# Attention products with v made feature-major in column halves of the array, and P divided by its sum before it is transposed

## The chip, the cores and the metric

The kernel runs on one core of a Trainium2 chip. The metric is the device time of one execution in microseconds (us). The engines are TensorE (PE in the profile, PEld its weight loads), VectorE (DVE), ScalarE (ACT), GpSimd (POOL) and SyncE (SP), which run their own queues of instructions in order and wait for each other by semaphores.

## What is computed

One sequence of 256 tokens, 1024 features wide, goes through three layers: a mixer that joins two attentions (MoBA with 8 heads, NSA with 8 heads in two groups), a squared-ReLU MLP, a forgetting attention ("fox") with 16 heads, a second MLP, and a hybrid layer (two SwiGLU blocks around differential attention and a state-space mixer). The change is in the first two mixers. Cut to what matters there, each head computes, with a bias table T that carries the causal mask:

```python
p = softmax(q @ k.T * scale + T)          # 256 x 256 per head, in two query blocks of 128
o = p @ v                                 # 256 x 64 per head
# NSA: three such products per head (compressed, selected, window keys),
#      o = g0 * o_cmp + g1 * o_slc + g2 * o_win, with gates g per token and head
# FoX: T[q, k] = cum[q] - cum[k], worked out in the kernel
y = concat(o of all heads) @ w_out
```

All of it is float32. Products with the streamed weights are made from a high and a low part of each factor (`whi`, `wlo`, and the halves of `xx`); the small products inside an attention are plain float32 matmuls, which the trace records as two passes each.

## The kernel before

A stream of weight pieces (`raw`, by SP's DMA queue) is split by ACT (`whi`, L387) and DVE (`wlo`, L388) while TensorE multiplies the piece before. A mixer is a generator `main` that makes its projections chunk by chunk, and a generator `attend2` that makes the attention; `drive` takes a step of the one and a step of the other, and a scheduler then orders each engine's queue by priorities that follow from that interleaving.

`attend2` treats heads by twos. There are 20 such pairs: 8 of NSA and 4 of MoBA in `even`, 8 in `fox`. A pair goes through these stages, each in another round of the loop:

- Age 0: four products of q and k into two PSUM banks (L214, `ps_b<-k,q`). The two heads' features lie in partitions 0 to 63 and 64 to 127, so the two heads use the two halves of the array's rows. DVE adds the table and finds the row's minimum of the negated scores (L542, into `S`), ACT makes the exponential and its sum (L545, `P` from `S`).
- Age 1: six transposes of P by TensorE (L555, three blocks of 128x128 a head, because the upper right block of 256x256 is masked), copied from PSUM to `PT` by ACT for the first head (L558) and by DVE for the second (L560).
- Age 2: products with v (L218, `ps_o<-v,PT`): P transposed is the stationary side, 128x128, and 64 columns of v move. Three such matmuls a head, six passes, so twelve passes a pair. The result is token-major: tokens in partitions, the heads side by side in a bank.

When all heads of a group are through, the sums are inverted, and DVE multiplies the outputs with them as it reads PSUM (`xn<-ps_o,mr`, L869 for NSA, where the gate is in the factor, L890 for MoBA, L1237 in `fox`; ten instructions of 128x512). For NSA, POOL adds the two parts (L878) and DVE the compressed one. The result is token-major and the output projection wants features in partitions, so `turn` transposes it by TensorE (L397, `ps_b<-cst,xn`, 32 blocks over both mixers) and splits it into high and low.

In `fox` the bias tables are built by POOL while the attention runs: for each of 16 heads four instructions (L1190, L1192, L1194, L1195) write a tile `S` out of a DMA-broadcast row (`T<-c_dram`) and the cumulated gates. `S` has four buffers and `P` five. `getT(h)` builds up to three tables ahead.

## Time and profile before

| | us |
|---|---|
| median of 3 runs (lowest, highest) | 1219.6 (1218.25, 1220.39) |
| the profiled execution | 1220.97 |
| its span in the trace | 1219.2 |
| busy in the span: PE, DVE, ACT, POOL | 1189.3, 785.6, 656.1, 119.0 |
| the first mixer's attention lies in | 36 to 142 of the span |
| the fox mixer's attention lies in | 367 to 475 of the span |

The span is what the trace covers from the first to the last instruction; the execution's own time has 1.8 us more around it. Ends of matmuls are modelled in the trace, and neighbours overlap, so what a group of matmuls costs is read from its first start to the start of what follows on TensorE, not from its duration.

### The profile page before, as it was taken

To read this page: it belongs to the slowest core of one execution; us is meant where nothing else is said; L and a number is where in the kernel's file an instruction comes from. 1 tells how busy PE (TensorE), PEld (TensorE's weight loads), DVE (VectorE), ACT (ScalarE), POOL (GpSimd) and SP (SyncE) were. 2 spreads that over 40 slices of the span, in tenths; PEclk is the share of its full clock that TensorE was granted. 3 is DMA by queue.
4 is the path that set the end of the run, shared out by engine and by line. 5 is a ranking of instruction groups with operands and counts; after the bars stand their busy time and mean duration, and the time that the engine had idled before them with its cause. 6 is when DMAs were issued, how large, how long until landed. Compare 5 with 4: busy or idle time off the path is not lost.

```text
span 1219.2 us, 17931 instructions
## 1 busy us (share of the span) xinstructions
PE 1189.3 (98%) x7008; PEld 1025.5 (84%) x7008; DVE 785.6 (64%) x1339; ACT 656.1 (54%) x1209; POOL 119.0 (10%) x182
## 2 busy tenths in 40 slices
PE   8999999999999999999999999999999999999997
PEld 6998888888887888888888888887988778988886
DVE  5676575656655546666676756576787876656563
ACT  6665454455454555545455555574664765555552
POOL 2001000000005220000002000002333120000000
PEclk9999999999999999999999999999999999999999
DMA  8645245555444424555563555562453235454550
GB/s 306 232 156 190 92 170 190 189 194 185 175 177 187 139 105 155 208 185 195 187 228 143 207 185 195 186 229 99 180 171 115 97 107 205 174 205 176 198 179 35
DMA packets 32533, 211.26 MB, mean 173 GB/s; under 512 B 3792, under 2 KB 4592, under 8 KB 8640
## 3 DMA queue, kind: packets, MB, share of 16 engines
q1 hardware_dynamic: 29040, 199.47, 46.0%
q0 software_dynamic: 3120, 10.38, 2.5%
q8 instruction: 55, 0.90, 0.3%
q10 hardware_dynamic: 288, 0.26, 0.1%
q14 instruction: 30, 0.25, 0.1%
HBM read 208.74 MB, written 1.09 MB: 172 GB/s over the span
## 4 chain that ended last, share of the span: by engine, by line
PE 84%; DVE 8%; ACT 4%; issue 2%; POOL 1%; DMA 1%; DVEq 0%; SPq 0%; ACTq 0%; POOLq 0%
PE ps_b L214 39%; PE ps_p L214 24%; PE ps_o L214 15%; DVE wlo L388 3%; PE ps_o L218 2%; ACT whi L387 1%; PE ps_p L397 1%; ACT P L545 1%; PE ps_b L397 1%; ACT xn L410 1%; PE ps_b L555 1%; DVE k L1326 1%; DVE xn L427 1%; POOL rs L416 1%; DMA gain<-in_mix_norm 1%
## 5 line engine op out<-in xcount | busy, mean ns | idle before, releaser
L388 DVE TENSOR_TENSOR wlo<-raw,whi 128x1024 fp32r<-128x1024 f32 (+1 forms) x365 | 447.8, 1245 | 245.6 <-ACT whi L387 244.7
L387 ACT ACTIVATE whi<-raw 128x1024 fp32r<-128x1024 f32 (+1 forms) x367 | 377.0, 1048 | 196.5 <-PE ps_p L214 90.4
L214 PE MATMUL ps_b<-xx,whi 128*128 128x512 f32 x1024 | 361.5, 394 | 0.0
L214 PE MATMUL ps_b<-xx,wlo 128*128 128x256 f32 x1024 | 289.0, 282 | 0.0
L214 PEld LDWEIGHTS ps_b<-xx,whi 128*128 128x128 f32 x1024 | 192.3, 188 | 43.8
L214 PEld LDWEIGHTS ps_b<-xx,wlo 128*128 128x128 f32 x1024 | 192.5, 188 | 1.7
L214 PE MATMUL ps_p<-xx,whi 128*128 128x256 f32 (+2 forms) x800 | 148.0, 287 | 1.2 <-ACT k L1324 0.7
L214 PEld LDWEIGHTS ps_p<-xx,whi 128*128 128x128 f32 (+2 forms) x800 | 121.9, 186 | 5.7 <-issue 3.1
L214 PE MATMUL ps_p<-xx,wlo 128*128 128x256 f32 x384 | 108.4, 282 | 0.0
L214 PE MATMUL ps_b<-whi,xx 128*128 128x256 f32 (+2 forms) x440 | 103.1, 321 | 0.0
L416 POOL TENSOR_TENSOR rs<-ms,mhalf 128x1 f32<-128x1 f32 x22 | 14.9, 675 | 825.9 <-DVE ms L423 825.9
L214 PE MATMUL ps_p<-whi,xx 128*128 128x512 f32 x232 | 83.8, 416 | 1.3 <-DVE xx L388 1.0
L214 PEld LDWEIGHTS ps_b<-whi,xx 128*128 128x128 f32 x440 | 73.2, 189 | 5.7 <-ACT xx L387 0.3
L214 PEld LDWEIGHTS ps_p<-xx,wlo 128*128 128x128 f32 x384 | 72.7, 189 | 0.0
L214 PE MATMUL ps_p<-whi,q 128*128 128x512 f32 x216 | 71.5, 391 | 0.0
L214 PE MATMUL ps_o<-whi,q 128*128 128x512 f32 x216 | 71.3, 391 | 0.0
L214 PE MATMUL ps_b<-wlo,xx 128*128 128x256 f32 (+2 forms) x220 | 70.6, 321 | 0.3 <-DVE wlo L388 0.2
L242 ACT ACTIVATE tB<-ps_b 128x256 f32<-128x256 f32 x128 | 47.7, 373 | 40.8 <-PE ps_b L214 40.8
L214 PE MATMUL ps_p<-whi,k 128*128 128x512 f32 x184 | 61.4, 394 | 0.0
L214 PE MATMUL ps_o<-whi,k 128*128 128x512 f32 x184 | 61.1, 393 | 0.0
L214 PEld LDWEIGHTS ps_p<-whi,xx 128*128 128x128 f32 x232 | 43.9, 191 | 15.0 <-issue 4.3
L387 ACT ACTIVATE k<-P 128x256 fp32r<-128x256 f32 x48 | 20.0, 418 | 64.2 <-DVE P L1054 36.8
(324 smaller groups left out, 1767.2 us busy)
## 6 DMA issues: line engine op xcount, KB each, us to landing
raw<-in_w_m SPq DMA_DIRECT2D x64, 1024.0 KB, 4.8
raw<-in_w_s SPq DMA_DIRECT2D x16, 1024.0 KB, 4.9
raw<-in_w_o SPq DMA_DIRECT2D x12, 1024.0 KB, 4.9
raw<-in_w_f1g SPq DMA_DIRECT2D x11, 1024.0 KB, 4.8
raw<-in_w_f1u SPq DMA_DIRECT2D x11, 1024.0 KB, 4.8
raw<-in_w_f1d SPq DMA_DIRECT2D x11, 1024.0 KB, 4.8
raw<-in_w_f2g SPq DMA_DIRECT2D x11, 1024.0 KB, 4.9
raw<-in_w_f2u SPq DMA_DIRECT2D x11, 1024.0 KB, 4.8
```

Source lines behind the costliest of these rows:

```text
L214: self.last_mm = self.nc.tensor.matmul(out, l, r, start=start, stop=stop)
L218: self.nc.tensor.matmul(out, l, r, start=start, stop=False, skip_group_check=True)
L242: nc.scalar.activation(tmp[:m], ps[:m, 256:512], AF.Copy)
L387: self.nc.scalar.activation(hi, src, AF.Copy)
L388: self.nc.vector.tensor_sub(lo, src, hi)
L397: i = self.nc.tensor.transpose(ps[:, k * 128:k * 128 + 128], src[:, (b + k) * 128:(b + k) * 128 + 128], self.ident)
L410: self.nc.scalar.activation(junk[:, h * 512:h * 512 + 512], halves[h], AF.Square, scale=1.0 / 32, accum_out=ss[:, h:h + 1])
L416: self.last_pow = self.nc.gpsimd.tensor_tensor(r, m, self.mhalf, op=OP.pow)
L427: self.nc.vector.scalar_tensor_tensor(dst, src, r, G, op0=OP.mult, op1=OP.mult)
L545: nc.scalar.activation(P[:, o:o + w], s[:, o:o + w], AF.Exp, scale=-1.0, bias=nm[:, j:j + 1], accum_out=J["sum"][:, j:j + 1])
L555: nc.tensor.transpose(b[:, c * 128:c * 128 + 128], P[:, c * 128:c * 128 + 128], self.ident)
L1326: nc.vector.scalar_tensor_tensor(xc[:, f], u[:, f, w:w + 256], cw[:, f, w:w + 1], xc[:, f], op0=OP.mult, op1=OP.add)
```

## The change

In both first mixers a pair's stages become:

- Age 0: as before, with DVE's minimum and ACT's exponential in place (`P` holds both; the two rings of buffers are joined to one of nine). The two heads' four sums lie in one tile `psum`; one RECIPROCAL on DVE makes `prec`. For NSA, POOL multiplies `prec` with the gate (128x4). Then four multiplications of P by its factor, two of 128x128 and two of 128x256: on POOL for the twelve pairs of `even`, on DVE for the eight of `fox`.
- Age 2 instead of 1: the transposes and copies.
- Age 3 instead of 2: products with v, v stationary (128x64), `PT` moving: 256 columns for the first block of keys (both query blocks at once) and 128 for the second. The first head writes PSUM partitions 0 to 63 and the second 64 to 127, which puts their stationary sides in the two halves of the array's columns. The order is: first head 256, second head 256, first head 128, second head 128. So four matmuls a pair, and the result is feature-major.

The outputs then need neither the division nor the turn: a new `take` splits them from PSUM straight into the high and low halves of `oT`. The compressed part of NSA accumulates in the same PSUM tile (four matmuls of 256 columns for two of 512). The ten `xn<-ps_o,mr`, POOL's two sums and the 32 transposes go. The rows of the output projection's weights are put in the new order of heads on the host before the launch. The diff, cut to its core:

```diff
-SB = 4
+PB = 9
+PAIR_T = 2
...
-            old = at.get(2)
+            old = at.get(PAIR_T + 1)
             if old:
                 flight.remove(old)
-                for J in old:
-                    pt, v, O = J["pt"], J["v"], J["O"]()
-                    s = slice(J["col"], J["col"] + 64)
-                    self.mmo(O[:, 0, s], pt[:, 0:128], v[0], J["first"])
-                    self.mmo(O[:, 1, s], pt[:, 128:256], v[0], J["first"])
-                    self.mmo(O[:, 1, s], pt[:, 256:384], v[1], False)
-                    if "after" in J:
-                        J["after"](pend)
+                O, c = old[0]["O"](), old[0]["col"]
+                for lo, n, i in ((0, 256, 0), (128, 384, 1)):
+                    for x, J in enumerate(old):
+                        o = O[64 * x:64 * x + 64, c // 512, c % 512 + lo:c % 512 + 256]
+                        self.mmo(o, J["v"][i], J["pt"][:, 256 * i:n], J["first"] and not i)
+                if "after" in old[0]:
+                    old[0]["after"]()
...
-                for J, b in zip(new, st):
+                sums = self.t([128, 2, 2], "psum", 3)
+                for x, (J, b) in enumerate(zip(new, st)):
...
-                    s = s0 if s0 is not None else self.t([128, 384], "S", SB)
-                    P = self.t([128, 384], "P", 5)
+                    P = J["P"] = s0 if s0 is not None else self.t([128, 384], "P", PB)
...
+                r = self.t([128, 2, 2], "prec", 3)
+                nc.vector.reciprocal(r, sums)
+                new[0]["norm"](r)
+                for x, J in enumerate(new):
+                    P = J["P"]
+                    for o, w, j in ((0, 128, 0), (128, 256, 1)):
+                        J["eng"].tensor_tensor(P[:, o:o + w], P[:, o:o + w],
+                                               r[:, x, j:j + 1].to_broadcast([128, w]), op=OP.mult)
             yield
-            for J in at.get(1, ()):
+            for J in at.get(PAIR_T, ()):
...
+    def take(self, O, oT, k, c, n=256):
+        m = n // 256
+        self.split(oT[:, k:k + m, 0:256], oT[:, k:k + m, 256:512],
+                   O[:, c // 512, c % 512:c % 512 + n].rearrange("p (k n) -> p k n", k=m))
...
         def nsa_sum():
-            for t in range(2):
-                o = no[t]
-                nc.gpsimd.tensor_tensor(o[:, :512], o[:, :512], o[:, 512:], op=OP.add)
-                ps = self.bank("p")
-                self.mm(ps, cpt[t][:120, :], vb[:120, :], True, True)
-                nc.vector.tensor_add(o[:, :512], o[:, :512], ps)
-                self.turn(o, oT, 4, t)
+            for j in range(4):
+                self.mmo(nO()[:, j // 2, j % 2 * 256:j % 2 * 256 + 256], vb[:120, j * 128:j * 128 + 128],
+                         w2[:120, 0:256], False)
+            for b in range(2):
+                self.take(nO(), oT, 4 + 2 * b, 512 * b, 512)
...
+                def norm(r, b=b, j=j):
+                    nc.gpsimd.tensor_tensor(r, r, gate.rearrange("p t (g j i) -> p j i g t", g=2, j=4)[:, j, b + 1],
+                                            op=OP.mult)
...
+                norm=lambda r: None, eng=nc.vector, first=h // 2 % 2 == 0, ev="av"[h % 2],
```

The scheduler then places the instructions anew. TensorE's queue at the third pair of NSA's products of q and k, where `xx` with `whi` and `wlo` are projections; before:

```order
L214 MATMUL ps_p<-xx,whi 128x256 x2
L214 MATMUL ps_p<-xx,wlo 128x256
L218 MATMUL ps_o<-v_157,PT 128x64 x6
L214 MATMUL ps_b<-k_156,q_155 128x128 x2
L214 MATMUL ps_b<-k_156,q_155 128x256 x2
```

and after:

```order
L215 MATMUL ps_p<-xx,wlo 128x256
L215 MATMUL ps_b<-k_156,q_155 128x128 x2
L219 MATMUL ps_o<-PT,v_157 64x256 x2
L219 MATMUL ps_o<-PT,v_157 64x128 x2
L215 MATMUL ps_b<-k_156,q_155 128x256 x2
L215 MATMUL ps_p<-xx,whi 128x256 x2
```

The pair's products with v, six matmuls that were whole, are four that stand inside the next pair's products of q and k. In 12 of the 20 pairs the two heads' 256 columns stand next to each other as here; in the other 8 something stands between them.

At the start of `fox`, TensorE's queue from the first pair's transposes (L555 before, L560 after) to the third pair's products of q and k; before:

```order
L555 MATMUL ps_b<-cst,P 128x128 x2
L214 MATMUL ps_p<-whi,xx 128x512
L218 MATMUL ps_o<-v_3232,PT 128x64 x6
L214 MATMUL ps_p<-whi,xx 128x512
L214 MATMUL ps_p<-wlo,xx 128x512
L214 MATMUL ps_p<-whi,xx 128x512
L214 MATMUL ps_b<-k_3231,q_3230 128x128
L218 MATMUL ps_o<-v_3232,PT 128x64 x6
```

and after:

```order
L215 MATMUL ps_p<-wlo,xx 128x512
L560 MATMUL ps_b<-cst,P 128x128 x5
L215 MATMUL ps_p<-whi,xx 128x512 x2
L219 MATMUL ps_o<-PT,v_3234 64x256
L560 MATMUL ps_b<-cst,P 128x128 x6
L215 MATMUL ps_p<-wlo,xx 128x512
L219 MATMUL ps_o<-PT,v_3234 64x256
L219 MATMUL ps_o<-PT,v_3234 64x128 x2
L215 MATMUL ps_p<-whi,xx 128x512
L215 MATMUL ps_b<-k_3233,q_3232 128x128 x2
```

Between the second pair's products of q and k and the first transpose there stood 48 passes of 256 columns, and now there stand 60 and four of 512; nine of 512 lie ahead of the third pair's products of q and k where six lay.

DVE's queue at the same place, behind the minima of the first two pairs (the last of them is the first row of each); before:

```order
L542 ISA S_3555,nm_3603<-ps_b_3592,S_3555 128x256
L542 ISA nm_3603 128x1
L560 COPY PT_3646<-ps_b_3642 128x384
L560 COPY PT_3695<-ps_b_3691 128x384
L388 TENSOR_TENSOR wlo_3730<-raw_3462,whi_3729 128x1024 x2
L542 ISA S_3604,nm_3751<-ps_b_3745,S_3604 128x128
```

and after:

```order
L542 ISA P_3556,nm_3609<-ps_b_3598,P_3556 128x256
L548 RECIPROCAL prec_3565<-psum_3534 128x4
L553 TENSOR_TENSOR P_3536<-P_3536,prec_3565 128x128
L553 TENSOR_TENSOR P_3536<-P_3536,prec_3565 128x256
L553 TENSOR_TENSOR P_3541<-P_3541,prec_3565 128x128
L553 TENSOR_TENSOR P_3541<-P_3541,prec_3565 128x256
L548 RECIPROCAL prec_3624<-psum_3603 128x4
L553 TENSOR_TENSOR P_3551<-P_3551,prec_3624 128x128
L553 TENSOR_TENSOR P_3551<-P_3551,prec_3624 128x256
L565 COPY PT_3687<-ps_b_3683 128x384
L389 TENSOR_TENSOR wlo_3723<-raw_3463,whi_3722 128x1024
```

Both pairs' multiplications (eight, of which six are shown) stand behind the minimum of the fourth head and ahead of the first copy of PT. POOL's queue goes on building tables through this stretch, as before.

## Rows read from the trace of the kernel before

**Rows 1.** The page: its head, the busy time of the engines, and the chain of work that ended last.

```profile
span 1219.2 us, 17931 instructions
PE 1189.3 (98%) x7008; PEld 1025.5 (84%) x7008; DVE 785.6 (64%) x1339; ACT 656.1 (54%) x1209; POOL 119.0 (10%) x182
...
PE 84%; DVE 8%; ACT 4%; issue 2%; POOL 1%; DMA 1%; DVEq 0%; SPq 0%; ACTq 0%; POOLq 0%
```

**Rows 2.** Windows: busy time of PE, PEld, DVE, ACT and POOL (us, with the number of instructions), granted clock, DMA share and GB/s in the two attention stretches.

```profile
36.00:142.00 106.00, 104.27 (x770) 90.78 (x769) 67.76 (x182) 58.85 (x156) 7.47 (x9) 1.00 0.44 156
367.00:475.00 108.00, 104.22 (x707) 89.97 (x705) 61.00 (x127) 55.79 (x128) 37.01 (x71) 0.98 0.38 137
```

**Rows 3.** Groups by line: the products with v on PE (48 of the 288 passes belong to the third mixer, which is not changed) and the turns of outputs (32 of the 64 go). Columns behind the bar: busy us, mean ns of one, then idle time just before.

```profile
L218 PE MATMUL ps_o<-v,PT 128*128 128x64 f32 x288 | 36.9, 272 | 1.5 <-ACT PT L558 1.5
L397 PE MATMUL ps_b<-cst,xn 128*128 128x128 f32 x64 | 10.0, 289 | 4.1 <-DVE xn L427 4.0
```

**Rows 4.** Timeline of PE in `fox`: a pair's products with v and its neighbours (start in us, duration with the modelled end, what, how many passes).

```profile
437.63 0.28 PE L214 MATMUL ps_p<-xx,wlo 128*128 128x256 f32 x1
437.75 1.45 PE L218 MATMUL ps_o<-v,PT 128*128 128x64 f32 x12
439.01 0.36 PE L214 MATMUL ps_p<-xx,whi 128*128 128x256 f32 x1
```

**Rows 5.** The same view: eight transposes of an output, and what follows.

```profile
455.46 1.04 PE L397 MATMUL ps_b<-cst,xn 128*128 128x128 f32 x8
456.25 0.47 PE L214 MATMUL ps_b<-whi,xx 128*128 128x512 f32 x1
```

**Rows 6.** The same view: a pair's products of q and k (eight passes, of two heads in the two halves of the rows), the projections before and behind, and six transposes of P.

```profile
427.46 0.40 PE L214 MATMUL ps_p<-xx,whi 128*128 128x256 f32 x2
427.70 0.28 PE L214 MATMUL ps_p<-xx,wlo 128*128 128x256 f32 x1
427.91 0.93 PE L214 MATMUL ps_b<-k,q 64*128 64x128 f32 x8
428.77 0.50 PE L214 MATMUL ps_p<-xx,whi 128*128 128x256 f32 x2
429.11 0.28 PE L214 MATMUL ps_p<-xx,wlo 128*128 128x256 f32 x1
...
430.30 0.82 PE L555 MATMUL ps_b<-cst,P 128*128 128x128 f32 x6
430.87 0.48 PE L214 MATMUL ps_p<-xx,whi 128*128 128x256 f32 x2
431.19 0.28 PE L214 MATMUL ps_p<-xx,wlo 128*128 128x256 f32 x1
```

**Rows 7.** The same view in `even`: six transposes, then products whose stationary side is only 60 or 30 columns wide.

```profile
58.20 0.82 PE L555 MATMUL ps_b<-cst,P 128*128 128x128 f32 x6
58.77 0.36 PE L214 MATMUL ps_p<-whi,gain 128*60 128x256 f32 x1
58.97 0.40 PE L214 MATMUL ps_p<-wlo,gain 128*30 128x256 f32 x2
59.20 0.28 PE L214 MATMUL ps_p<-whi,gain 128*60 128x256 f32 x1
```

**Rows 8.** One line's instructions, with the lowest, median and highest duration in ns, first and last start: splits by DVE that read two tiles of SBUF, POOL's first two instructions of a table, and DVE's copies of PT.

```profile
L388 DVE TENSOR_TENSOR wlo<-raw,whi x365: 731/1220/4497, 9.8 to 1192.0; 128x1024 fp32r<-128x1024 f32 x181, 128x560 fp32r<-128x560 f32 x1, 128x1120 fp32r<-128x1120 f32 x1
L388 DVE TENSOR_TENSOR k<-P,k x48: 414/425/426, 194.7 to 1188.6; 128x256 fp32r<-128x256 f32 x48
L388 DVE TENSOR_TENSOR whi<-raw,whi x2: 292/292/293, 353.9 to 858.1; 128x128 fp32r<-128x128 f32 x2
L1190 POOL TENSOR_TENSOR S<-T,cq x16: 388/398/1388, 380.4 to 432.7; 128x128 f32<-128x128 f32 x16
L1192 POOL TENSOR_TENSOR S<-T,cq x16: 602/608/1592, 381.3 to 434.0; 128x256 f32<-128x256 f32 x16
L560 DVE COPY PT<-ps_b x20: 495/555/559, 53.2 to 451.5; 128x384 f32<-128x384 f32 x20
```

**Rows 9.** Groups by line: ACT's exponentials and the readout of their sums (mean ns behind the comma).

```profile
L545 ACT ACTIVATE P<-S,nm 128x256 f32<-128x256 f32 x40 | 19.9, 497 | 2.7 <-DVE nm L542 2.5
...
L545 ACT ACTIVATION_READ_ACCUMULATOR P<-S,nm 128x1 f32 x80 | 15.0, 188 | 0.0
```

**Rows 10.** Timeline of DVE at the start of `fox`: the first and the last of the minima of the first four heads.

```profile
382.34 0.29 DVE L542 CUSTOM_DVE_ANT_0 S<-ps_b,S 128x128 f32<-128x128 f32 x1 [1.28 <-POOL S L1194]
...
388.02 0.42 DVE L542 CUSTOM_DVE_ANT_0 S<-ps_b,S 128x256 f32<-128x256 f32 x1
```

**Rows 11.** Timeline of PE at the same place: the last projection before the wait, the first transpose, and the third pair's products of q and k.

```profile
381.60 0.28 PE L214 MATMUL ps_p<-xx,wlo 128*128 128x256 f32 x1
383.33 0.30 PE L555 MATMUL ps_b<-cst,P 128*128 128x128 f32 x1 [1.45 <-DVE nm L542]
...
391.78 0.49 PE L214 MATMUL ps_b<-k,q 64*128 64x128 f32 x2
```

**Rows 12.** Windows of one us at the same place, columns as in Rows 2; the granted clock is the third figure from the end.

```profile
384.00:385.00 1.00, 0.43 (x3) 0.23 (x3) 0.73 (x4) 0.52 (x3) 1.00 (x4) 0.95 1.04 401
385.00:386.00 1.00, 0.91 (x5) 0.94 (x6) 0.15 (x1) 0.58 (x2) 1.00 (x3) 0.50 0.36 148
387.00:388.00 1.00, 1.00 (x7) 1.00 (x6) 0.30 (x2) 0.39 (x3) 1.00 (x4) 0.50 0.08 33
388.00:389.00 1.00, 1.00 (x5) 0.53 (x3) 0.90 (x3) 0.95 (x5) 1.00 (x3) 0.85 0.00 0
```

**Rows 13.** Timeline: a DVE split of two SBUF tiles while POOL builds tables without a break, and the last POOL instruction of that stretch.

```profile
391.61 4.50 DVE L388 TENSOR_TENSOR wlo<-raw,whi 128x1024 fp32r<-128x1024 f32 x1
394.57 0.45 POOL L1195 TENSOR_TENSOR S<-S,cst 128x128 f32<-128x128 f32 x1
```

**Rows 14.** Timeline: two DVE splits, and POOL's table instructions beside them, some us later.

```profile
402.10 3.02 DVE L388 TENSOR_TENSOR wlo<-raw,whi 128x1024 fp32r<-128x1024 f32 x2 [0.28 <-ACT whi L387]
402.09 0.40 POOL L1190 TENSOR_TENSOR S<-T,cq 128x128 f32<-128x128 f32 x1
402.44 1.59 POOL L1192 TENSOR_TENSOR S<-T,cq 128x256 f32<-128x256 f32 x1
404.00 1.44 POOL L1194 TENSOR_TENSOR S<-S,cst 128x128 f32<-128x128 f32 x1
405.40 0.46 POOL L1195 TENSOR_TENSOR S<-S,cst 128x128 f32<-128x128 f32 x1
```

More of the change, by code (lines that the diff above doesn't have):

```diff
@@ L509, in attend2 @@
         nc = self.nc
-        flight, pend, todo = [], [], list(pairs)
-        while todo or flight or pend:
-            run, pend = pend, []
+        flight, todo = [], list(pairs)
+        while todo or flight:
             for J in flight:
@@ L895, in even @@
-        for h in range(8):
-            g = h // 4
-            s = slice(g * 64, g * 64 + 64)
-            Th = (self.back(T[:, 8 + h, 0:128]), self.back(T[:, 8 + h, 0:256]), None)
-            for b in range(2):
-                nsa[b].append(dict(
-                    ready=lambda: "nv" in F, qk=[(nq[s, h % 4], kk[s, b])], T=lambda Th=Th: Th,
-                    v=[nv[:, t, b * 128 + g * 64:b * 128 + g * 64 + 64] for t in range(2)],
-                    O=nO[b], col=h * 64, first=h == 0, sum=nsum[:, b, h], ev="av"[h % 2]))
+        nO, mO = self.once(self.opair), self.once(self.opair)
@@ L908, in even @@
-        for h in range(8):
-            s = slice(h % 2 * 64, h % 2 * 64 + 64)
-            Th = (self.back(T[:, h, 0:128]), self.back(T[:, h, 0:256]), None)
-            need = ("mv", "m%d" % (h // 4))
-            if h % 2 == 0:
-                jobs.append([])
-            jobs[-1].append(dict(
-                ready=lambda need=need: all(n in F for n in need), qk=[(mq[s, h // 2], mk[s, h // 2])],
-                T=lambda Th=Th: Th, v=[mv[:, t, h * 64:h * 64 + 64] for t in range(2)], O=mO, col=h * 64,
-                first=h == 0, sum=msum[:, h], ev="av"[h % 2]))
@@ new lines, in even @@
+        jobs[-1][0]["after"] = lambda: F.add("nO1")
+        for j in range(4):
+            jobs.append([])
+            for g in range(2):
+                h = 2 * j + g
+                s = slice(g * 64, g * 64 + 64)
+                Th = (self.back(T[:, h, 0:128]), self.back(T[:, h, 0:256]), None)
+                jobs[-1].append(dict(
+                    ready=lambda j=j: "mv" in F and "m%d" % (j // 2) in F, qk=[(mq[s, j], mk[s, j])],
+                    T=lambda Th=Th: Th, v=[mv[:, t, h * 64:h * 64 + 64] for t in range(2)], O=mO, col=j * 256,
+                    norm=lambda r: None, eng=nc.gpsimd, first=j % 2 == 0, ev="av"[g]))
+            jobs[-1][0]["after"] = lambda j=j: self.take(mO(), oT, j, j * 256)
@@ L1227, in fox, with done @@
         O = [self.once(self.opair) for _ in range(2)]
[L1228 removed]
         self.pre_out, self.late_turns = [], []
[L1231 to L1246 removed]
+        def done(i):
+            self.take(O[i // 4](), oT, i, i % 4 * 256)
+            if i == 3:
+                F.add("half")
         jobs = []
@@ L1252, in fox @@
                 ready=lambda h=h: h // 4 in F, qk=[(q[s, h // 2], k[s, h // 2])], T=lambda h=h: getT(h),
-                v=[v[:, t, h * 64:h * 64 + 64] for t in range(2)], O=O[h // 8], col=h % 8 * 64,
-                first=h % 8 == 0, sum=sums[:, h], ev="av"[h % 2]))
-        jobs[7]["after"] = lambda pend: out(0)(pend)
-        jobs[15]["after"] = lambda pend: out(1)(pend)
+                v=[v[:, t, h * 64:h * 64 + 64] for t in range(2)], O=O[h // 8], col=h // 2 % 4 * 256,
+                norm=lambda r: None, eng=nc.vector, first=h // 2 % 2 == 0, ev="av"[h % 2],
+                after=lambda i=h // 2: done(i)))
         self.drive(main(), self.attend2([jobs[i:i + 2] for i in range(0, 16, 2)]))
```

115 lines of the change are left out of this document (37 added, 78 removed).

## The prediction

> **What bounds the kernel now.** I read the page first, then the two attention stretches in windows, then TensorE's own rows there. TensorE is busy for 1189.3 of 1219.2 us and makes up 84% of the chain that ended last [rows 1]. In the two stretches that the change touches it is busy for 104.27 of 106 us and for 104.22 of 108, while DVE has 67.76 and 61.00, ACT less, and POOL 7.47 and 37.01 [rows 2]. So the change gains what it takes off TensorE's queue, and costs what it makes TensorE wait. Work added to DVE and POOL is free as long as the result is there when TensorE's next instruction needs it. The place to look is where TensorE already waits: the start of `fox`.
>
> **Basis of the sum.** The profiled execution took 1220.97 us, of which its span is 1219.2, and lies 1.4 above the median of 1219.6. I make the sum of differences against that execution and take it off the median.
>
> **Products with v, before.** All 288 passes are busy for 36.9 us, but ends overlap [rows 3]; from first start to the start of what follows, a pair's twelve passes take 439.01 - 437.75 = 1.26 us [rows 4]. Other pairs are a little longer, so I take 1.3, or 26 us for 20 pairs. Each pass streams only 64 columns but takes 0.105 us.
>
> **Turns removed.** Eight transposes take 456.25 - 455.46 = 0.79 us, 0.099 each [rows 5]. 32 of them go: -3.2 us. Their DVE and ACT work lay beside TensorE and is replaced by the splits from PSUM; I count nothing for it.
>
> **Products with v, after.** No row shows two stationary sides in the two column halves at once, so I bound it. What plain float32 columns cost is in six transposes of 128 columns, 0.57 us [rows 6], so 0.095 to 0.11 for 128 and about 0.22 for 256. A pair now streams, for each head, two passes of 256 and two of 128: 0.44 + 0.22 = 0.66 us. If the two heads run one behind the other, a pair costs 1.32, and nothing is saved against 1.3. If they run together, it costs 0.66. The nearest row is the products of q and k, whose two heads sit in the two halves of the rows: they stream the same columns (128 and 256, two passes each, two heads) and would need 1.32 one behind the other, yet 428.77 - 427.91 = 0.86 us is all they take [rows 6], some 0.2 of it at the change into and out of the row halves (0.21 from the last projection's start at 427.70 to the first pass, where 0.12 is usual, and 0.34 for two passes behind, where 0.24 is usual). So halves of rows do run together; I take the same for columns. The 12 pairs whose 256s are neighbours save 0.64 each, -7.7. In the 8 others the 256s don't meet: 0.44 + 0.44 + 0.22 = 1.1, saving 0.2 each, -1.6. Together **-9.3**, bounded by 0 and -12.8 (all 20 joined).
>
> Does the change of array shape itself cost anything? Going into and out of row halves costs 0.2 [rows 6]. Going from six transposes to stationary sides of 60 and 30 columns does not: the six take 58.77 - 58.20 = 0.57 and the three passes behind 59.20 - 58.77 = 0.43, which is 0.08 more than 3 x 0.117 [rows 7]; behind the six transposes of [rows 6] two full-width passes take 431.19 - 430.87 = 0.32, 0.08 more than usual too. So the 0.08 belongs to the transposes, and I take 0 for columns. [...] What does cost: the scheduler now puts products with v between the products of q and k, which makes 28 stretches of row halves out of 26: 2 x 0.2 = **+0.4**.
>
> **The multiplications in `even`.** POOL takes 0.39 us for 128x128 and 0.60 for 128x256 [rows 8], so four cost 1.98 us a pair. The work between a pair's products of q and k and its transposes is 60 projection passes of 0.117 (two take 0.24 in [rows 6]) and two more pairs' q and k of 0.86: 8.7 us. The chain needs four minima (1.4 by [rows 10], 0.29 and 0.42 each twice), the last exponential and readout 0.7 [rows 9], an inversion and the gate (under 1), and 1.98: 5.1, or 7.6 if POOL also waits for two DVE splits of 1.22 [rows 8]. So they are covered: 0, and with some delay of DVE's splits behind POOL, and the end of the mixer, where cover runs out, **+0.4** for both mixers' ends together. If the cover were gone, each pair would cost up to 2 us.
>
> **The start of `fox`.** Here there is no cover. POOL builds tables without a pause, and the first four heads' minima wait for them: from 382.34 to 388.44 [rows 10]. TensorE runs out of projections at 381.9, and the third pair's q and k come at 391.78 [rows 11]. Now DVE has to do an inversion and eight multiplications behind the last of these minima (its order of instructions above). Two tiles of SBUF in, 128x128 costs 0.29 and 128x256 0.42 [rows 8], so a pair costs 1.43 alone. But DVE and POOL hinder each other when both read SBUF tiles: with 1.22 usual, a split took 1.5 each beside POOL, and POOL's 0.60 became 1.59 [rows 14]. There they alternate, one instruction of each. Alternating, DVE waits for a POOL instruction of 0.39 to 0.60 [rows 8], or for the rest of one, ahead of each multiplication, and the eight end at 394.35 instead of 391.5; I put TensorE's new order against this. It has 12 more projection passes and four of 512 columns ahead of the first transpose, so it arrives at 383.9; the first transpose starts at 389.2, the first pair's last at 391.6, the second pair's last at 394.5; with the copy of PT (0.55, [rows 8]) and the first pair's last products the third pair's q and k start at 395.9. In the old order, with the three projections of 512 columns (0.23 each, two passes of 256) that are now ahead of them, that would be 392.5. So **+3.6**, with the 0.2 of the products with v that is counted above. The wait is longer than the one before, and in that one the granted clock fell to 0.50 for about 3.3 us from 385 on [rows 12]; half speed while a few us of work are due costs **+1.2**. DVE's splits behind the multiplications and the third and fourth pairs, which POOL's tables meet as well, **+0.8** (0 to 2).
>
> The sum: -3.2 - 9.3 + 0.4 + 0.4 + 3.6 + 1.2 + 0.8 = -6.1, so 1219.6 - 6.1 = **1213.5 us**.
>
> **The rivals.**
> Halves of columns take turns. The products with v then save nothing: +9.3, so 1222.8, slower than before. For it speaks that the row halves are fed from different partitions and that no row here shows two column tiles at once; against it, that the 60-wide group behaves like a full one [rows 7]. It decides the sign: the result is slower than before if a pair still takes about 1.27 us or more, and within 0.2% above 1.0. [...]
>
> DVE is shut out by POOL. One split was not served in turn at all: begun at 391.61 it took 4.50 us and ended 1.1 after POOL's last instruction of the stretch [rows 13]. Four splits alternated and one did not. If the multiplications at the start of `fox` fare like that one, the first pair's end waits for POOL's ring of nine buffers to fill, to about 396.5, and everything behind is about 5.5 us later: 1219.0.
>
> [...]
>
> DVE is served first. Then the eight multiplications end at 391.7, the start costs +0.7 instead of 3.6, and the clock and what follows cost 1.0 less: 1209.6.
>
> [...]
>
> **How the numbers follow.** About 0.2%, 2.4 us, is what a measurement of this kernel can tell from no change. Forecast 0.38; DVE served first 0.13; shut out 0.17; drain 0.07; turns 0.19; two together 0.06. Faster by over 0.2% (under 1217.2) are the forecast, the served-first case, and half of the shut-out and drain cases' spread, whose centres lie at the edge: 0.60. Same: the rest of those and a third of the turns case: 0.20. Slower: 0.20. The range of 8 in 10 runs from 1208.5, which leaves out the best of the served-first case, to 1224, which leaves out the two together.
>
> **What would show it.** In the new trace, the two heads' 256-column passes start some ns apart, and a joined pair takes 0.66 to the next instruction (right) or 1.3 (turns). [...] At the start of `fox` the eight L553 multiplications last 0.6 to 0.9 us each (alternating), 0.3 to 0.4 (served first), or one of them several us (shut out), and TensorE waits for P at the first transposes for about 5 us. In `even` no transpose waits for POOL. The forecast is wrong if the transposes wait in the middle of either mixer, or if DVE's splits come late enough to stop projections.

## The result and the profile after

| | before | after |
|---|---|---|
| median (lowest, highest), us | 1219.7 (1218.25, 1220.39) | 1229.0 (1226.40, 1229.75) |
| the profiled execution, its span | 1220.97, 1219.2 | 1226.40, 1224.6 |

Four runs of each give a ratio of 1.0061, with a 95% interval from 1.0048 to 1.0074: slower, where faster was forecast, and above the range. The medians differ by 9.3 us and the profiled executions by 5.4, since that of before is above its median and that of after is the fastest of its four; the slower ones of after have a lower mean granted clock (0.988 to 0.989, where it has 0.993), and no trace shows where they lose the rest. The page of the kernel after, to be read beside [rows 1]:

```profile
span 1224.6 us, 17852 instructions
PE 1183.9 (97%) x6900; PEld 1006.2 (82%) x6900; DVE 795.5 (65%) x1377; ACT 657.4 (54%) x1215; POOL 147.8 (12%) x236
PE   8999999999995999999999999999999999999997
PEclk9999999999997999999999999999999999999999
PE 83%; DVE 7%; ACT 3%; POOL 3%; issue 2%; DMA 1%; SPq 0%; POOLq 0%; DVEq 0%; ACTq 0%
```

TensorE does 108 passes fewer, is busy for 5.4 us less, and the span is 5.4 us longer. One slice of forty has fallen, to 5 tenths busy and a clock of 7. The windows of the two attention stretches, as in [rows 2], say which it is, and the waits of TensorE in the whole span (line waited at, who was waited for, us, times, longest) say for what:

```profile
36.00:142.00 106.00, 102.36 (x718) 81.74 (x717) 64.47 (x183) 60.26 (x159) 34.77 (x61) 1.00 0.44 153
367.00:475.00 108.00, 94.29 (x603) 75.14 (x604) 67.11 (x150) 49.93 (x122) 35.85 (x70) 0.94 0.36 128
```

```profile
PE ps_b L560 <- DVE P L553: 12.7, 1, 12.7
...
PE ps_o L219 <- DVE PT L565: 1.6, 2, 1.2
```

In the first mixer TensorE is nearly as busy as before (102.36 after 104.27); in `fox` TensorE is busy for 94.29 of 108 us where it was 104.22, and one wait of 12.7 us, at the first transposes, stands out. To see where time went, I use the same instructions as milestones in both traces: the first products of q and k, the last four passes of the second pair's in `fox`, the third pair's first pass, and the first turn of the norm behind `fox`. Before (the third is in [rows 11]):

```profile
39.80 0.93 PE L214 MATMUL ps_b<-k,q 64*128 64x128 f32 x8
...
375.29 0.70 PE L214 MATMUL ps_b<-k,q 64*128 64x256 f32 x4
...
468.02 0.66 PE L397 MATMUL ps_p<-cst,xn 128*128 128x128 f32 x4 [0.37 <-DVE xn L427]
```

and after:

```profile
39.09 0.93 PE L215 MATMUL ps_b<-k,q 64*128 64x128 f32 x8
...
372.56 0.70 PE L215 MATMUL ps_b<-k,q 64*128 64x256 f32 x4
...
400.01 0.92 PE L215 MATMUL ps_b<-k,q 64*128 64x128 f32 x6
...
473.48 0.65 PE L398 MATMUL ps_p<-cst,xn 128*128 128x128 f32 x4 [0.36 <-DVE xn L428]
```

| stretch | before | after | |
|---|---|---|---|
| up to the first products of q and k | 39.80 | 39.09 | -0.7 |
| from there to the second pair's of `fox` (the first mixer and its MLP) | 335.5 | 333.5 | -2.0 |
| from there to the third pair's (the start of `fox`) | 16.5 | 27.5 | +11.0 |
| from there to the norm (the rest of `fox`) | 76.2 | 73.5 | -2.8 |

The four add up to +5.5, which is all of the difference in span. The first mixer gains 2.0, the rest of `fox` 2.8, and the start of `fox` loses 11.0. Some 0.7 of the last two is work that changed sides: three projections of 512 columns more now lie ahead of the third pair's. The lengths hardly change from run to run: the same kernel again gave 333.5 and, for all of `fox`, 101.5 after 100.9, while the start of the first row moved between 38.6 and 41.6 over all kernels. So in the experiments I compare these lengths (with the last two joined, as `fox`) beside the medians.

What the start of `fox` looks like on DVE (groups of one line share a row), then TensorE's rows, and windows with PE, PEld, DVE, ACT and POOL:

```profile
385.67 0.17 DVE L548 RECIPROCAL prec<-psum 128x4 f32<-128x4 f32 x1
385.88 9.17 DVE L553 TENSOR_TENSOR P<-P,prec 128x128 f32<-128x128 f32 x4
394.97 0.17 DVE L548 RECIPROCAL prec<-psum 128x4 f32<-128x4 f32 x1
```

```profile
L553 DVE TENSOR_TENSOR P<-P,prec x32: 279/418/8296, 385.9 to 456.5; 128x128 f32<-128x128 f32 x16, 128x256 f32<-128x256 f32 x16
```

```profile
380.88 0.63 PE L215 MATMUL ps_p<-whi,xx 128*128 128x512 f32 x2
394.23 0.48 PE L560 MATMUL ps_b<-cst,P 128*128 128x128 f32 x1 [12.72 <-DVE P L553]
```

```profile
386.00:394.00 8.00, 0.00 (x0) 0.00 (x0) 8.00 (x1) 0.66 (x3) 8.00 (x19) 0.50 0.00 0
394.00:400.00 6.00, 5.77 (x25) 3.67 (x25) 4.73 (x11) 2.68 (x5) 4.38 (x9) 0.71 0.00 0
```

The first multiplication begins at 385.88 and takes 8296 ns, where the median is 418. From 386 to 394 DVE has one instruction in work and POOL nineteen, one behind the other; TensorE has none. The multiplication ends at 394.18, when POOL, whose last instruction ended at 394.03, has stopped for want of a free buffer; POOL's next instruction waits for a transpose:

```profile
395.64 0.41 POOL L1172 TENSOR_TENSOR P<-T,cq 128x128 f32<-128x128 f32 x1 [1.62 <-PE ps_b L560]
```

The granted clock is 0.50 in the wait and 0.71 on the mean of the six us behind it.

The products with v, to be held against [rows 4]: a joined pair, then a split pair's first head and the rest, with TensorE's neighbours.

```profile
122.51 0.28 PE L215 MATMUL ps_p<-xx,wlo 128*128 128x256 f32 x1
122.72 0.87 PE L219 MATMUL ps_o<-PT,v 128*64 128x256 f32 x8
123.52 0.50 PE L215 MATMUL ps_p<-whi,xx 128*128 128x512 f32 x1
```

```profile
83.19 0.65 PE L219 MATMUL ps_o<-PT,v 128*64 128x256 f32 x2
83.77 0.33 PE L215 MATMUL ps_p<-whi,gain 128*60 128x256 f32 x1
...
84.61 0.86 PE L219 MATMUL ps_o<-PT,v 128*64 128x256 f32 x6
85.40 0.66 PE L560 MATMUL ps_b<-cst,P 128*128 128x128 f32 x4
```

A joined pair takes 123.52 - 122.72 = 0.80 to the next start, where 0.66 was forecast, and 0.21 lies ahead of it where 0.12 is usual. A split pair takes 0.58 + 0.79, with 0.09 ahead of each part: 1.55, more than the 1.3 before.

### The profile page after: what moved, and what is told of

It is laid out like the page before. It is cut to its first block, busy times and chain, and to the rows that moved or that the text cites. A ratio compares the mean times of both kernels' runs of the same rounds, so it can differ in the third digit from the quotient of the medians.

```text
span 1224.6 us, 17852 instructions
## 1 busy us (share of the span) xinstructions
PE 1183.9 (97%) x6900; PEld 1006.2 (82%) x6900; DVE 795.5 (65%) x1377; ACT 657.4 (54%) x1215; POOL 147.8 (12%) x236
## 4 chain that ended last, share of the span: by engine, by line
PE 83%; DVE 7%; ACT 3%; POOL 3%; issue 2%; DMA 1%; SPq 0%; POOLq 0%; DVEq 0%; ACTq 0%
PE ps_b L215 38%; PE ps_p L215 25%; PE ps_o L215 15%; DVE wlo L389 2%; PE ps_o L219 2%; ACT whi L388 1%; PE ps_p L398 1%; PE ps_b L560 1%; ACT xn L411 1%; DVE P L553 1%; POOL rs L417 1%; ACT P L545 1%; DVE xn L428 1%; DMA P<-in_oh 1%; DMA T<-c_dram 1%
## 5 line engine op out<-in xcount | busy, mean ns | idle before, releaser
L244 DVE TENSOR_TENSOR P<-ps_b,tB 128x256 f32<-128x256 f32 x128 | 53.6, 418 | 5.7 <-ACT tB L243 5.7
```

What stands on the lines that cost most here:

```text
L244: nc.vector.tensor_add(dst, ps[:m, :256], tmp[:m])
```

## The experiments

**Theory.** The loss is DVE shut out by POOL at the start of `fox`: a DVE instruction that reads two tiles of SBUF isn't served while POOL goes from one table instruction to the next, and DVE's order puts all the multiplications where POOL has a long run. **Rivals:** the multiplications are too much work for DVE, wherever they stand; or the loss is that of the products with v, whose halves of columns cost as much as they save.

| kernel | median (lowest, highest; runs), us | ratio to before [95%] | first mixer and MLP | `fox` |
|---|---|---|---|---|
| before | | | 335.5 | 92.7 |
| again (after, once more) | 1227.5 (1226.4, 1229.5; 5) | 1.0060 [1.0048, 1.0072] | 333.5 | 101.5 |
| wide | 1228.8 (1228.2, 1230.1; 5) | 1.0070 [1.0057, 1.0083] | 336.4 | 100.8 |
| joined | 1223.8 (1221.0, 1225.7; 10) | 1.0020 [1.0009, 1.0031] | 332.6 | 99.5 |
| even_only | 1217.5 (1216.3, 1219.9; 7) | 0.9975 [0.9964, 0.9986] | 333.5 | 92.8 |
| fox_nomul | 1223.3 (1222.1, 1224.8; 10) | 1.0018 [1.0009, 1.0028] | 333.5 | 97.1 |
| fox_act | 1224.1 (1218.0, 1227.7; 12) | 1.0027 [1.0012, 1.0042] | 333.5 | 93.2 |
| fox_tables_wait | 1230.4 (1223.9, 1233.3; 6) | 1.0072 [1.0049, 1.0094] | 333.4 | 105.0 |
| fox_break | 1222.2 (1219.6, 1223.7; 12) | 1.0008 [0.9999, 1.0018] | 333.6 | 96.9 |
| fox_early | 1218.8 (1216.3, 1224.7; 10) | 0.9986 [0.9970, 1.0001] | 333.6 | 92.6 |
| even_joined | 1216.3 (1214.4, 1218.4; 6) | 0.9957 [0.9943, 0.9970] | 332.5 | 92.8 |
| joined_early | 1216.3 (1213.7, 1218.9; 6) | 0.9959 [0.9943, 0.9974] | 331.2 | 90.4 |

The last two columns are lengths between milestones in each kernel's profiled execution, as above. The medians of the kernel before in these sessions were 1220.9 to 1221.5. The sessions were on three chips; by the ratios, each to the kernel before of its own session, what a kernel gains on the repeat is up to 1.4 us more than by the medians, which the text goes by.

**The changed kernel again** (again), as the measure for the others.

> The changed kernel once more, to see how far its time spreads and whether the wait at the start of the fox mixer is there in every execution. If DVE's first multiplication of P is shut out by POOL as long as POOL builds tables (theory A), its profile shows one L553 of about 8 us again and TensorE's wait of 12 to 13 us, and the time is 1226 to 1230. If that wait was an accident of the one profiled execution (theory B), L553 lasts under 1 us in this profile and the time scatters towards 1218.

It came out as in the first session, and its first multiplication took 8299 ns in place of 8296. The shut-out isn't chance.

**Only the first mixer changed** (even_only), `fox` as before the change (its old `attend2`, `S` and `P` rings and jobs stand beside the new ones).

> The first mixer as changed, the fox mixer as before (token-major products, division behind them, turns), and the two rings of buffers as before, of which the changed first mixer takes one each for the two heads. In the traces so far the first mixer ends 2.7 us earlier and the fox mixer loses 8.2. If the loss is in the fox mixer alone, this is faster than before by 2 to 3 us (0.998). If the loss sits elsewhere or the profiled executions mislead, it is at 1.003 or above.

0.25% faster than before. All of the loss lies in `fox`.

**No multiplications in `fox`** (fox_nomul).

```diff
...
                 for x, J in enumerate(new):
+                    if J["eng"] is nc.vector:
+                        continue
                     P = J["P"]
...
```

> The multiplications of P by its factor are left out in the fox mixer (its rows are then not divided by their sums); the inversions stay. With nothing on DVE between minima and transposes that reads two SBUF tiles, TensorE's wait at the first transposes should fall from 12.7 us to 3 or less and the time to 1217 (1215 to 1220). If it stays above 1223, other instructions (DVE's splits behind POOL) make the loss.

I had expected the loss to go with the multiplications, and half of it stayed: `fox` is 4.4 longer than before, where the repeat's is 8.8. The time is above the 1223 from which on other instructions were to make the loss. TensorE's longest wait and DVE's rows in this kernel:

```profile
PE ps_o L219 <- DVE xx L389: 7.4, 1, 7.4
```

```profile
389.18 8.96 DVE L389 TENSOR_TENSOR wlo<-raw,whi 128x1024 fp32r<-128x1024 f32 x1 [1.42 <-ACT whi L388]
398.07 0.41 DVE L389 TENSOR_TENSOR xx<-ps_o,xx 128x256 fp32r<-128x256 f32 x1
```

The next DVE instruction with two SBUF inputs, a split of a weight piece, is shut out in their place, for 8.96 us. Behind it on DVE stands the first pair's `take`, and the second pair's products with v write the PSUM tile that this reads, so TensorE waits for a split that it doesn't need. This speaks against the rival of too much DVE work: with less work, the same kind of wait is there. Before the change nothing of the kind stood behind the split of [rows 13]: outputs were read from PSUM only when all heads of a group were through.

**The multiplications on ACT** (fox_act).

```diff
...
+                        if J["eng"] is nc.scalar:
+                            nc.scalar.activation(P[:, o:o + w], P[:, o:o + w], AF.Copy, scale=r[:, x, j:j + 1])
...
-                norm=lambda r: None, eng=nc.vector, first=h // 2 % 2 == 0, ev="av"[h % 2],
+                norm=lambda r: None, eng=nc.scalar, first=h // 2 % 2 == 0, ev="av"[h % 2],
```

> In the fox mixer alone, ACT instead of DVE multiplies P by its factor (an activation with a scale per row). Theory A (DVE and POOL exclude each other, POOL's unbroken queue wins): ACT is not shut out, each multiplication lasts 0.4 to 0.5 us, TensorE's wait at the first transposes falls from 12.7 to under 5 us, and the time to 1220 (1218 to 1223). Theory C (the multiplications as such, placed behind four minima and ahead of the transposes, are what makes TensorE wait): the wait shrinks by less than 3 us and the time stays above 1225.

The profiled execution has a wait of 4.6 us at the first transposes, and a shut-out at the next split again, shorter:

```profile
389.38 5.37 DVE L389 TENSOR_TENSOR wlo<-raw,whi 128x1024 fp32r<-128x1024 f32 x1
```

The times scatter over 10 us, and the profiled execution is the fastest of them, so the median isn't explained by that trace; at 1224.1 it lies between the two theories' ranges and decides nothing. What holds is that ACT isn't shut out: its four multiplications take 1.49 us a pair beside POOL's tables in that execution.

**POOL's run broken by data** (fox_tables_wait). From the fifth head's table on, POOL reads a copy of the gates that DVE makes behind the second pair's multiplications, and `getT(3)` builds nothing ahead.

```diff
...
+            g = cq
+            if h >= 4:
+                if not cq2:
+                    cq2.append(self.t([128, 2, 16], "cq2"))
+                    self.later(nc.vector.tensor_copy(cq2[0], cq), self.last_mul)
+                g = cq2[0]
...
-            build(h + 1)
-            if h % 2:
-                build(h + 2)
+            if h != 3:
+                build(h + 1)
+                if h % 2:
+                    build(h + 2)
...
```

> The multiplications stay on DVE, but POOL builds only the tables of the first four heads and then waits: the tables of heads 4 to 15 read a copy of the cumulated gates that DVE makes behind the second pair's multiplications. Theory A: no L553 at the start lasts over 0.6 us, the first transposes start 7 to 8 us earlier relative to the third pair's minima, and the time is 1222 (1219 to 1225). Theory C: 1228 or more, since the multiplications stand where they stood and the tables come later.

The start is mended (multiplications of 0.28 to 0.42, a wait of 4.7), but POOL's run now starts later, and the third pair's multiplications meet it:

```profile
404.04 9.94 DVE L553 TENSOR_TENSOR P<-P,prec 128x128 f32<-128x128 f32 x4
```

The first of these took 9.07 us. The two waits for L553 are 12.6 together, and nothing is gained: the time, 1230.4, lies where the rival was to be, but by another way than the rival's. The shut-out goes with POOL's run, not with the place.

**A POOL instruction that reads nothing, behind each table** (fox_break). The orders of all four engines are otherwise those of the changed kernel.

```diff
...
+            if Ts:
+                self.later(i, self.brk)
...
-            nc.gpsimd.tensor_tensor(s[:, 256:384], s[:, 256:384], self.mask, op=OP.add)
+            i = nc.gpsimd.tensor_tensor(s[:, 256:384], s[:, 256:384], self.mask, op=OP.add)
+            self.brk = nc.gpsimd.memset(self.t([128, 48], "brk", 1), 0.0)
+            self.later(self.brk, i)
...
```

> The changed kernel with one short POOL instruction that reads nothing (a memset of 128x48 into a tile of its own, about 0.15 us) behind each of the 16 bias tables of fox; VectorE's and POOL's orders are otherwise the same. If VectorE is kept out for as long as POOL goes from one SBUF-reading instruction straight to the next, the first instruction that reads nothing lets it in: the first multiplication lasts at most about 2.6 us in place of 8.3, TensorE's wait at the first transposes falls from 12.7 to between 4 and 7 us, and the time to 1219 to 1223. The rival is that it is POOL being busy at all that keeps VectorE out, up to the point where POOL itself waits: then the multiplication lasts 8.3 us or more, and the time is that of the changed kernel, 1227 to 1230.

This tells most, since no engine's order differs otherwise. DVE's four multiplications of the first pair and POOL's rows beside them:

```profile
386.65 3.16 DVE L553 TENSOR_TENSOR P<-P,prec 128x128 f32<-128x128 f32 x4
```

```profile
387.02 0.45 POOL L1178 TENSOR_TENSOR P<-P,cst 128x128 f32<-128x128 f32 x1
387.43 0.45 POOL L1179 TENSOR_TENSOR P<-P,cst 128x128 f32<-128x128 f32 x1
387.83 0.13 POOL L1180 MEMSET brk<- 128x48 f32 x1
387.92 0.40 POOL L1172 TENSOR_TENSOR P<-T,cq 128x128 f32<-128x128 f32 x1
388.27 0.80 POOL L1176 TENSOR_TENSOR P<-T,cq 128x256 f32<-128x256 f32 x1
389.03 0.50 POOL L1178 TENSOR_TENSOR P<-P,cst 128x128 f32<-128x128 f32 x1
```

The first multiplication begins at 386.65, is passed by two table instructions, and ends at 388.03, 0.2 after the start of the memset of 0.13 us. The next ones take 0.64 to 0.70, one for each of POOL's, and POOL's rows grow (L1176 to 0.80, where about 0.61 is usual). The wait at the transposes is 6.0, and `fox` is 4.6 shorter than in the repeat:

```profile
PE ps_b L560 <- DVE P L553: 6.0, 1, 6.0
```

2 us of POOL work in all buy 5 us. The rival of this run's expectation, that POOL being busy at all shuts DVE out, falls. Whether it is the missing read or the other kind of instruction that lets DVE in was not tried.

**Another order of DVE** (fox_early). A pair's multiplications stand ahead of the next pair's minima. POOL's order is unchanged; a few of TensorE's and ACT's instructions in `fox` come in another order than in the changed kernel, since the scheduler placed them anew.

```diff
...
+                mark = getattr(self, "last_mul", None) if new[0]["eng"] is nc.vector else None
...
-                        nc.vector.tensor_tensor_reduce(
+                        i = nc.vector.tensor_tensor_reduce(
...
+                        if mark is not None:
+                            self.later(i, mark)
...
+                if new[0]["eng"] is nc.vector:
+                    self.last_mul = m
...
```

> Only DVE's order in the fox mixer: a pair's multiplications come ahead of the next pair's minima instead of behind them, so that the first one meets POOL about 5 us into its run of table instructions rather than 7.7. In the profiles so far a DVE instruction of two SBUF tiles waited 4.5 to 9 us if it was the first to meet a run of POOL instructions 6.9 us old or older, and one POOL instruction if the run was under 5.4 us old. If age decides, no L556 at the start lasts over 1 us and the time is 1221. If any run of tables shuts DVE out until it pauses, the first L556 lasts over 10 us, the second pair's minima wait behind it, and the time is 1229 or more.

```profile
382.86 2.31 DVE L556 TENSOR_TENSOR P<-P,prec 128x128 f32<-128x128 f32 x4
385.09 0.28 DVE L543 CUSTOM_DVE_ANT_0 P<-ps_b,P 128x128 f32<-128x128 f32 x1
...
388.02 2.11 DVE L556 TENSOR_TENSOR P<-P,prec 128x128 f32<-128x128 f32 x4
```

```profile
PE ps_b L565 <- DVE P L556: 2.7, 1, 2.7
```

Three us earlier the same multiplications take turns with POOL: four in 2.31, 0.55 to 0.70 each, about the 0.6 to 0.9 that the prediction had put for them. The wait is 2.7, `fox` is as long as before the change, and the time falls by 8.7 against the repeat. No work has been taken away, so the rival of too much DVE work falls. With fox_break this shows that the loss at the start of `fox` is the shut-out; what decides whether it comes is another question, taken up at the end.

**Products with v without halves of columns** (wide). v of both heads is stationary, 128 wide.

```diff
...
-                        o = O[64 * x:64 * x + 64, c // 512, c % 512 + lo:c % 512 + 256]
-                        self.mmo(o, J["v"][i], J["pt"][:, 256 * i:n], J["first"] and not i)
+                        o = O[:, c // 512, c % 512 + lo:c % 512 + 256]
+                        self.mmo(o, J["w"][i], J["pt"][:, 256 * i:n], J["first"] and not i and not x)
...
```

> The products with v use the full width: the stationary side is v of both heads (128 columns), and the two heads' P follow one another into the same PSUM partitions, so that each head's product is added to the other's (the output is not that of the reference; everything behind runs as before). This takes away both the overlap of the two heads and any pause at a change of the array's shape. If halves of columns overlap but each entry and exit costs 0.1 us, a pair whose products are neighbours takes 1.31 to 1.35 us instead of 0.80 with 0.09 ahead of it, a pair whose products are apart 1.35 instead of 1.37 with 0.18, and the time rises by 12 x 0.45 - 8 x 0.2 = 3.8 to 1233. If the halves gain nothing, the time falls or stays at 1229.

```profile
125.58 0.29 PE L215 MATMUL ps_p<-xx,wlo 128*128 128x256 f32 x1
125.70 1.47 PE L219 MATMUL ps_o<-PT,v 128*128 128x256 f32 x8
126.93 0.48 PE L215 MATMUL ps_p<-whi,xx 128*128 128x512 f32 x1
```

This pair, with none but projections beside it, takes 1.23 and has the usual 0.12 ahead of it. So two halves of columns do run together (0.80), and the 0.09 ahead and some 0.14 behind (0.80 less the estimate of 0.66) belong to the half-wide tiles. In the first mixer the halves are worth 2.9 us, by the lengths; in `fox`, which waits anyway, the kernel without them is 0.7 shorter than the repeat. Over the whole kernel they are worth only 1.3 by the medians, where I had expected 3.8. By itself the time of 1228.8 lies where the expectation put halves that gain nothing; that they run together is read from the rows.

**All 20 pairs side by side** (joined). The second head, whose copy of PT comes last, goes first, and the four matmuls are kept together.

```diff
...
-                    for x, J in enumerate(old):
+                    for x, J in ((1, old[1]), (0, old[0])):
...
+                        if x == 1:
+                            if i == 0:
+                                self.later(m, old[0]["cp"])
+                        else:
+                            self.later(m, prev)
...
```

> The change, with the products with v of all 20 pairs side by side: TensorE's order is set so that the first head's 256 columns follow the second head's at once (8 pairs had other work between). If a separated pair costs 1.37 us and 0.18 ahead of it where a joined one costs 0.80 and 0.09, 8 pairs save 0.66 each, 5 us less than the change, 0.996 of it, less what the wait for both copies of PT adds. If TensorE's time there is covered by other waits, under 2 us.

3.7 us less than the repeat, where 5 less the waits for PT was expected, 0.9 of it in the first mixer and 2.0 in `fox`; the shut-out is still there (8301 ns, a wait of 12.7). The two losses are separate.

**The first mixer alone, joined** (even_joined), and **both repairs together** (joined_early: joined and the order of fox_early).

> The first mixer alone as changed, with all its 12 pairs' products with v side by side; fox as before the change. Against even_only (1217.5) the split pairs of this mixer gain about 0.7 us each, so 1214.5 to 1217. It tells, beside joined_early, whether the change is worth anything in fox once the shut-out is gone: if fox with the change is still no better than fox before, joined_early isn't faster than this kernel; by the sum of passes (four of eight fox pairs side by side already, 16 turns gone) joined_early should be 1 to 3 us the faster.

> Both repairs in one kernel: all 20 pairs' products with v side by side (as in joined), and in fox VectorE's order with a pair's multiplications ahead of the next pair's minima (as in fox_early). If the two losses are independent, as I hold, their gains against the changed kernel add: joined gave -3.7 us and fox_early -8.7, so about 1227.5 - 12.4 = 1215, range 1212.5 to 1218, a ratio to the kernel before of about 0.996. The rival is that the time which joined saves was taken from TensorE's slack around the wait and is lost again once the wait is gone, or that the shut-out comes back at another instruction because the products stand earlier: then 1218 or more.

Both are 0.4% faster than the kernel before. The two repairs together gain 11.2 on the repeat, where alone they gained 3.7 and 8.7, so they nearly add. By the medians the two kernels are as good as each other, where I had expected the second to lead by 1 to 3 us (that expectation counts four of the eight `fox` pairs as side by side already; three were). In the profiled executions `fox` is 2.4 us shorter with the change (90.4 after 92.8), so its removed passes are worth something once the shut-out is gone; but this is about as much as the times of one kernel scatter, and the medians don't show it. In joined_early every pair's products with v read as these two do:

```profile
447.97 0.87 PE L524 MATMUL ps_o<-PT,v 128*64 128x256 f32 x8
448.77 0.73 PE L215 MATMUL ps_b<-whi,xx 128*128 128x512 f32 x2
...
450.20 0.87 PE L524 MATMUL ps_o<-PT,v 128*64 128x256 f32 x8
451.00 0.50 PE L215 MATMUL ps_b<-wlo,xx 128*128 128x512 f32 x1
```

## Why the prediction was wrong

**The start of `fox`: the step that failed.** "There they alternate, one instruction of each" was taken for the eight multiplications from four splits that alternated [rows 14], against one that didn't [rows 13]. They fared like the one: the first lasted 8.3 us, and TensorE waited for 12.7 where about 5 was forecast. The forecast put the third pair's q and k at 395.9, 4.1 after the 391.78 of before (0.7 of it the projections now ahead of them), and 1.2 for the clock, 5.3 in all; the rival "DVE is shut out by POOL" added 5.5, so 10.8; measured +11.0. Mechanism, place and price of that rival were right, and its chance of 0.17 was too low. The two groups of rows differ in a thing that I hadn't read: the split of [rows 13] met POOL 11.2 us after its run had begun (at 380.4, the first start in [rows 8]), the first of those in [rows 14] 3.5 us after (at 398.56). The multiplications meet the same long run as the split of [rows 13] did, and after 7.7 us. The row to weigh by was the one in whose situation the new instructions would be, even though it stays open what in that situation decides.

**Products with v: mechanism right, the cost of the change left out.** Halves of columns run together, as forecast (0.80 a joined pair, where full-wide ones take 1.23), and the rival of halves that take turns falls. But "I take 0 for columns" failed, the second step that did: a change into the half-wide tiles and out of them again costs 0.09 + 0.14 = 0.23, and with 28 stretches (12 joined pairs and two for each of 8 split ones) that is 6.4; at the 0.2 read at the halves of rows [rows 6] it is 28 x 0.2 = 5.6. The step read [rows 7], where tiles of 60 and 30 columns come after full ones without a pause, and took these for half-wide ones. The chance of 0.07 was put on a "drain" at this change; no run shows what the array does there, only the 0.09 ahead and some 0.14 behind. The terms as they came out: from first start to next start, the 20 pairs' products took 26.4 us before (26 forecast) and 23.8 after; with 28 x 0.09 ahead, 26.3, so the -9.3 shrank to nearly nothing. 3.2 of the 23.8 are pairs whose two heads' 256s don't start together though they stand side by side (four of the twelve), and one stretch that begins at a granted clock of 0.50 (0.78 for a split pair's first head, where 0.58 is usual). In the longest of them, in the first mixer, the second head's copy of PT on DVE is late:

```profile
52.00 0.65 PE L219 MATMUL ps_o<-PT,v 128*64 128x256 f32 x2
53.85 0.86 PE L219 MATMUL ps_o<-PT,v 128*64 128x256 f32 x6 [1.21 <-DVE PT L565]
```

In joined_early the same 20 pairs take 20 x 0.80 and 20 x 0.09, 17.8: -8.6, about the forecast's -9.3. With every pair joined that saving is there on the passes; but a joined pair needs both copies of PT, and TensorE waits 4.1 us for them ahead of five pairs, where before the change such waits came to 1.5.

**Both rivals at once.** The shut-out and the cost of the change were given 0.17 and 0.07 as if each came alone; "two together" paired either only with the halves that take turns. Both would have been 1213.5 + 5.5 + 5.6 = 1224.6, with 0.2 for each of 28 stretches, above the upper end of the range. Nothing in the profile made one exclude the other. As measured, the start of `fox` missed by 5.7 and the products with v by 9.2, 14.9 of the 15.5 by which the median lies above the forecast; between the profiled executions the miss is 11.5. Two smaller figures were off: the chance of "faster" is 0.63 by its own parts, not 0.60, and the row halves come in 31 stretches in the trace, where there were 28, not in 28 out of 26 (+0.6 for +0.4).

**What was right.** The turns left without a trace elsewhere; the multiplications on POOL in the first mixer are covered (0.4 us of waits for them in all); the first mixer gained, though 2.0 and not the 7.6 of its share of the sum (16 turns, nine joined and three split pairs, less 0.4), for the reasons above. The rest of `fox` gained 2.8 (0.7 of it the projections that moved ahead), though its multiplications and splits meet POOL too, for which +0.8 was counted.

## What to carry to other kernels

When work is put on an engine that another one hinders, look at the order in which it meets the other's long runs, not only at the cost of an instruction beside it: here eight multiplications of 0.3 to 0.4 us make a start of 27.5 us in one order of DVE's queue and of 19.1 in another, and a short instruction that reads nothing behind each of POOL's tables cut 5 us of it. If such a cost has two values in the trace, price the new work by the row that stands in the same situation, and price rivals that don't exclude each other together. For matmuls on half-wide tiles, keep those of a pair side by side: joined they save a third of the time that they took (0.89 a pair, where it was 1.3), less what the wait for both heads' data costs, and split they lose (1.55 a pair, where it was 1.3).

## What the runs showed of the hardware

A DVE instruction with two SBUF inputs that meets POOL's run of SBUF-reading instructions is in some cases passed by 7 to 20 of them (it lasted 8.3 us in four kernels, 4.5 in three, and 5.4, 8.96 and 9.07 in one each). It was let in where POOL paused (in after it ended 0.15 us behind POOL's last instruction of the run), in fox_break at an instruction that reads nothing (a memset of 0.13 us), and in two cases (fox_nomul, fox_act) at the first instruction of a table though POOL went on (that instruction took 1.46 and 1.48 us, where 0.40 is usual). DVE's minima, which read PSUM and one SBUF tile, took their usual 0.29 and 0.42 beside POOL, and ACT's four multiplications took 1.49 us beside it in fox_act.

What decides between being shut out and taking turns stays open. Sorted by how long POOL's run in `fox` had lasted when the first DVE instruction of this kind began inside it, the cases of all thirteen traces fall apart: eleven began 6.9 to 11.9 us into a run and were passed by (in fox_break up to the memset), and 24 began at 5.0 us or less and took turns. Once turns had begun, they went on in the same run. But the time since DVE's own last instruction of this kind sorts them as well, and without asking which is the first: of the 137 that began inside such a run, the eleven came 7.1 us or more after it, and all others 6.3 or less, some of them over 20 us into a run. Neither was varied alone (fox_early shortened both), so the traces don't tell the two apart, and a third thing may stand behind them.

Two half-wide matmuls of 256 columns in the two halves of the array's columns start 6 ns apart and take 0.80 with their 128s, where full-wide ones take 1.23.
